# Four units of w_in beside the splitting of x, loaded with it in nine pieces, with squares summed alongside and two raw weight buffers

## The chip, the cores and the metric

The kernel runs on one core of one Trainium2 chip. The metric is the time of one execution on the device in microseconds, the median of three runs. Five engines work side by side and meet only at semaphores: TensorE (PE; PEld is its weight load), VectorE (DVE), ScalarE (ACT), GpSimd (POOL) and SyncE (SP), whose queue issues nearly all loads.

## What is computed

One layer of a decoder for 288 tokens: 256 of a prompt and 8 times 4 of samples, with D = 2048. All of it is fp32. Cut to what matters:

```python
h = rmsnorm(x, g_pre_mix)                 # x * rsqrt(mean(x*x) + eps) * g
z = h @ w_in                              # columns: q | k | v | g_ret | B | C | h_conv | gate_a | gate_b
q, k, v, g_ret, gb, gc, hc, gate_a, gate_b = split(z)
o = retention(rotary(q), rotary(k), v, state_ret)      # 8 heads, per-head decay
y_a = (silu(g_ret) * groupnorm(o)) @ p_ret
y_b = (gb * causal_dwconv(gc * hc)) @ p_conv
m = sigmoid(gate_a) * y_a + sigmoid(gate_b) * y_b
x = x + rmsnorm(m @ w_o, g_post_mix)
h2 = rmsnorm(x, g_pre_ffn)
f = (gelu(causal_dwconv(h2 @ w_up) + b) * (h2 @ w_gate)) @ w_down
x = x + rmsnorm(f, g_post_ffn)
```

## The kernel before

Tokens lie along the free dimension, 288 wide; D lies on partitions, 16 blocks of 128 (k). A *unit* is 128 output columns of a weight matrix, 1 MB, over 16 blocks. To keep fp32 accuracy each operand is split into a high part (fp32r) and a low part, and `mm3` (L118 to 121) makes three matmuls of 128x128 by 128x288 for each block: 48 a unit.

`wunit` (L98 to 114) brings one unit: SP loads it into a tile of the tag raw (the pool has three buffers), ScalarE casts the high part (L110), VectorE subtracts for the low part (L111), in halves of 1024 columns; the tags wh and wl hold three halves each. `gemm` runs mm3 over them, into a PSUM bank of the tag acc (three banks; the tag r has five, L87). `project` (L241) is a unit of w_in, unless its sum already lies in `pre`.

The front (L198 to 239) loads x into xt in five pieces, and with each the same rows of three units, FIRST = (0, 1, 16): two blocks of q and one of k. For each piece ScalarE makes hop's high part x*g (L215), VectorE its low part (L216), the weights are split (L221, L222), and TensorE multiplies. ScalarE squares x (L234), GpSimd adds the squares up (L237, L239) into the first of the tiles acca. Then `rstd_tokens` (three matmuls of the sum with a column, L167; GpSimd's power, L171) starts the first norm, unit 17 is projected, and `rstd_bcast` (VectorE's diagonal L180, fp32 matmuls with a tile of ones, L182, named strb) with ScalarE's copy gives rstd1. The norm's rstd is applied behind the products: cos and sin are multiplied by it (L283, L284), and `v_unit` (L317) multiplies its PSUM sum by it into vT, a product of 256 and one of 32 columns four times over (L322, L323), which frees the bank.

Later come the eight heads with their states (POOL and SP load and store them), w_o (L730, with x1 loaded anew at L693 and 694), the second norm with three first units of w_up and w_gate beside it (L738 to 756; two have tiles of their own for the parts, the third uses `wunit`), and w_down (L869 to 880). A scheduler sets each engine's order of work from its own estimate of times, except in blocks with a hand-written order; on an engine, instructions run in that order.

Of the kernel before, what the change touches and what calls it, by code (L numbers as in the profile page):

```python
# [17 lines left out]
P = 128  # L18
# [58 lines left out]
def tile_hybrid_step(ctx: ExitStack, tc: tile.TileContext, a, o):  # L77
# [20 lines left out]
    def wunit(src, pieces, step=1024):  # L98
        u = n_unit[0]
        n_unit[0] += 1  # L100
        raw = wp.tile([P, 2048], F32, tag="raw", name=f"raw{u}")
        nc.sync.dma_start(out=raw[:, : sum(pieces)], in_=src)
        parts = []
        at = 0
        for i, n in enumerate(pieces):
            wh = wp.tile([P, 1024], F32R, tag="wh", name=f"wh{u}_{i}")
            wl = wp.tile([P, 1024], F32R, tag="wl", name=f"wl{u}_{i}")
            for c in range(0, n, step):
                to, of = slice(c, min(c + step, n)), slice(at + c, at + min(c + step, n))
# [50 lines left out]
    LAST = N - P  # L160
    CHUNKS = ((0, 0, P, 0), (1, P, P, 0), (2, LAST, NS, P - NS))

    def rstd_tokens(sq, name):

        st = psum("r", f"st_{name}")
        for c, at, _, _ in CHUNKS:
            T.matmul(st[:, c : c + 1], sq[:, at : at + P], mean, start=True, stop=True)  # L167
        tt = cp.tile([P, 3], F32, tag="stt", name=f"stt_{name}", bufs=2)
        V.tensor_scalar(out=tt, in0=st[:, 0:3], scalar1=EPS, scalar2=None, op0=ALU.add)
        r = cp.tile([P, 3], F32, tag="str", name=f"str_{name}", bufs=2)  # L170
        G.tensor_tensor(out=r, in0=tt, in1=mhalf[:, 0:3], op=ALU.pow)  # L171
        return r

    def rstd_bcast(r, name):

        dg = cp.tile([P, N], F32, tag="stdg", name=f"stdg_{name}")
        rb = psum("r", f"strb_{name}")
        for c, _, n, skip in CHUNKS:
            to = slice(P * c, P * c + n)
            V.tensor_scalar(out=dg[:, to], in0=ident[:, skip:], scalar1=r[:, c : c + 1],  # L180
                            scalar2=None, op0=ALU.mult)
            T.matmul(rb[:, to], ones, dg[:, to], start=True, stop=True)  # L182
        return rb[:, :N]


    hstack = ExitStack()
    hp = Pool(hstack.enter_context(tc.tile_pool(name="hp", bufs=1)))
    hops = [hp.tile([P, 2, N], F32R, name=f"hop{k}") for k in range(KT)]
    acca = [hp.tile([P, N], F32, name=f"acca{k}") for k in range(KT)]
    rstd1 = hp.tile([P, N], F32, name="rstd1")  # L190


    warm = cp.tile([P, 4], F32, name="warm")
    S.activation(warm, mhalf, AF.Tanh)
    g1 = const("g1", [P, KT])
    pre = {}
    sq_acc = acca[0]
    with tc.tile_pool(name="xp", bufs=1) as xpool:  # L198
        xp = Pool(xpool)
        FIRST = (0, 1, 16)  # L200
        xt = xp.tile([P, KT, N], F32, name="xt")
        raws = [xp.tile([P, 2048], F32, name=f"raw_s{u}") for u in FIRST]
        whs = [xp.tile([P, 2048], F32R, name=f"wh_s{u}") for u in FIRST]
        wls = [xp.tile([P, 2048], F32R, name=f"wl_s{u}") for u in FIRST]
        accs = [psum("r" if i == 0 else "acc", f"a_s{u}") for i, u in enumerate(FIRST)]
        pieces = ((0, 2), (2, 4), (4, 8), (8, 12), (12, 16))
        for k0, k1 in pieces:
            nc.sync.dma_start(out=xt[:, k0:k1, :], in_=a["xT"][:, k0:k1, :])
            w = slice(P * k0, P * k1)
            for raw, u in zip(raws, FIRST, strict=True):  # L210
                nc.sync.dma_start(out=raw[:, w], in_=a["w_in"][u][:, w])
        for k0, k1 in pieces:
            w = slice(P * k0, P * k1)
            for k in range(k0, k1):
                S.activation(hops[k][:, 0, :], xt[:, k, :], AF.Copy, scale=g1[:, k : k + 1])  # L215
                V.scalar_tensor_tensor(  # L216
                    out=hops[k][:, 1, :], in0=xt[:, k, :], scalar=g1[:, k : k + 1],
                    in1=hops[k][:, 0, :].bitcast(F32), op0=ALU.mult, op1=ALU.subtract,
                )
            for i, raw in enumerate(raws):  # L220
                S.copy(whs[i][:, w], raw[:, w])  # L221
                V.tensor_tensor(out=wls[i][:, w], in0=raw[:, w], in1=whs[i][:, w].bitcast(F32),  # L222
                                op=ALU.subtract)
# [6 lines left out]
        for k0, k1 in pieces[1:]:  # L230
            if k0 == 2:
                k0 = 0
            sq = xp.tile([P, 4, N], F32, tag="sq", name=f"sq{k0}", bufs=1)
            S.square(sq, xt[:, k0:k1, :])  # L234
            for j in range(4):
                if k0 == 0 and j == 0:
                    G.tensor_copy(out=sq_acc, in_=sq[:, 0, :])  # L237
                else:
# [602 lines left out]
    for half in range(2):  # L841
# [189 lines left out]
```

## Time and profile before

| | us |
|---|---|
| median of three runs | 2555.78 (2554.3 to 2555.91) |
| the profiled execution | 2555.46 |
| its span, first to last instruction | 2553.4 |
| TensorE busy | 2536.8 (99%) |
| VectorE busy | 1534.6 (60%) |
| ScalarE busy | 1067.8 (42%) |
| GpSimd busy | 90.2 (4%) |
| mean granted clock of TensorE | 0.999 |

The span begins with the first instruction and ends with the last; the profiled execution's own time lies 2.1 us above it. A busy share says how much of the span an engine had an instruction running, not whether it ran at full pace; matmuls overlap in the pipeline, so the distance between two starts, not a duration, is what one costs.

### The profile page before, as it was taken

The numbers are of one execution on the slowest core, as the hardware profiler recorded it, in microseconds if no ns is written. First come the engines' busy times: TensorE is split into PE (matmuls) and PEld (weight loads), VectorE is DVE, ScalarE is ACT, GpSimd is POOL, SyncE is SP. The second block draws the span as 40 slices with busy tenths as digits, with TensorE's granted clock in tenths as the row PEclk, the third lists the DMA queues.
The fourth block names the chain that finished last, engine by engine and source line by source line (L and its number), as shares of the span: only waits on it lengthen the run. The fifth ranks groups of instructions, "written<-read, shape, count | busy, mean of one in ns | idle before, by whom it ended". The sixth has DMA issues, their size and how long they took to land.

```text
span 2553.4 us, 44916 instructions
## 1 busy us (share of the span) xinstructions
PE 2536.8 (99%) x18864; PEld 2480.2 (97%) x18864; DVE 1534.6 (60%) x2339; ACT 1067.8 (42%) x1463; POOL 90.2 (4%) x256
## 2 busy tenths in 40 slices
PE   8999999999999999999999999999999999999998
PEld 8999999999999999999999999999999999999998
DVE  7565656666666666555555554477666446666654
ACT  5444434443444433333333333454444334444443
POOL 2000000000000000000000000021000000000001
PEclk9999999999999999999999999999999999999999
DMA  7465765657565664444444445544444454444645
GB/s 270 174 237 202 245 223 217 242 199 257 207 256 209 237 225 182 165 165 165 168 165 166 166 166 214 207 168 165 166 165 152 167 174 173 166 165 166 222 163 183
DMA packets 90347, 493.06 MB, mean 193 GB/s; under 512 B 11040, under 2 KB 13856, under 8 KB 47776
## 3 DMA queue, kind: packets, MB, share of 16 engines
q1 hardware_dynamic: 88416, 480.74, 52.7%
q0 software_dynamic: 1728, 9.44, 1.0%
q8 instruction: 148, 2.42, 0.4%
q14 instruction: 55, 0.45, 0.1%
HBM read 440.04 MB, written 50.10 MB: 192 GB/s over the span
## 4 chain that ended last, share of the span: by engine, by line
PE 97%; DVE 1%; DMA 1%; issue 0%; ACT 0%; SPq 0%; DVEq 0%; ACTq 0%
PE a_d L121 4%; PE a_d L119 4%; PE a_d L120 4%; PE a_gate L121 4%; PE a_gate L120 4%; PE a_gate L119 4%; PE a_up L121 4%; PE a_up L120 3%; PE a_up L119 3%; PE a_p L119 3%; PE a_g L119 3%; PE a_g L120 3%; PE a_gt L121 3%; PE a_p L121 3%; PE a_g L121 3%; PE a_gt L119 3%
## 5 line engine op out<-in xcount | busy, mean ns | idle before, releaser
L111 DVE TENSOR_TENSOR wl<-raw,wh 128x1024 fp32r<-128x1024 f32 (+2 forms) x776 | 906.2, 1168 | 683.6 <-ACT wh L110 679.5
L110 ACT CAST wh<-raw 128x1024 fp32r<-128x1024 f32 (+2 forms) x776 | 778.1, 1003 | 1279.0 <-PE a_d L120 154.2
L119 PE MATMUL a_d<-fop,wh 128*128 128x288 f32 x704 | 207.9, 295 | 0.0
L120 PE MATMUL a_d<-fop,wh 128*128 128x288 f32 x704 | 207.0, 294 | 0.0
L121 PE MATMUL a_d<-fop,wl 128*128 128x288 f32 x704 | 206.7, 294 | 0.0
L119 PE MATMUL a_gate<-h2op,wh 128*128 128x288 f32 x688 | 203.2, 295 | 0.0
L120 PE MATMUL a_gate<-h2op,wh 128*128 128x288 f32 x688 | 203.0, 295 | 0.0
L121 PE MATMUL a_gate<-h2op,wl 128*128 128x288 f32 x688 | 202.8, 295 | 0.0
L119 PE MATMUL a_up<-h2op,wh 128*128 128x288 f32 x672 | 198.4, 295 | 0.0
L120 PE MATMUL a_up<-h2op,wh 128*128 128x288 f32 x672 | 198.3, 295 | 0.0
L121 PE MATMUL a_up<-h2op,wl 128*128 128x288 f32 x672 | 198.2, 295 | 0.0
L119 PE MATMUL a_p<-yop,wh 128*128 128x288 f32 x512 | 153.1, 299 | 0.0
L119 PE MATMUL a_g<-hop,wh 128*128 128x288 f32 x512 | 152.6, 298 | 0.0
L120 PE MATMUL a_g<-hop,wh 128*128 128x288 f32 x512 | 151.7, 296 | 0.0
L119 PE MATMUL a_v<-hop,wh 128*128 128x288 f32 x512 | 151.2, 295 | 0.0
L119 PE MATMUL a_gt<-hop,wh 128*128 128x288 f32 x512 | 151.1, 295 | 0.0
L120 PE MATMUL a_gt<-hop,wh 128*128 128x288 f32 x512 | 150.9, 295 | 0.0
L120 PE MATMUL a_p<-yop,wh 128*128 128x288 f32 x512 | 150.8, 294 | 0.0
L120 PE MATMUL a_v<-hop,wh 128*128 128x288 f32 x512 | 150.6, 294 | 0.0
L121 PE MATMUL a_gt<-hop,wl 128*128 128x288 f32 x512 | 150.6, 294 | 0.0
L121 PE MATMUL a_p<-yop,wl 128*128 128x288 f32 x512 | 150.5, 294 | 0.0
L121 PE MATMUL a_g<-hop,wl 128*128 128x288 f32 x512 | 150.4, 294 | 0.0
(303 smaller groups left out, 6627.5 us busy)
## 6 DMA issues: line engine op xcount, KB each, us to landing
raw<-in_w_in SPq DMA_DIRECT2D x173, 1024.0 KB, 4.9
raw<-in_w_down SPq DMA_DIRECT2D x64, 704.0 KB, 4.0
raw<-in_w_up SPq DMA_DIRECT2D x43, 1024.0 KB, 4.8
raw<-in_w_gate SPq DMA_DIRECT2D x43, 1024.0 KB, 4.8
st<-in_state SPq DMA_DIRECT2D x64, 512.0 KB, 5.0
out_ret_s<-st SPq DMA_DIRECT2D x64, 512.0 KB, 6.6
raw<-in_p_ret SPq DMA_DIRECT2D x32, 1024.0 KB, 4.8
raw<-in_p_conv SPq DMA_DIRECT2D x16, 1024.0 KB, 4.7
```

What stands on the lines that cost most here:

```text
L110: S.copy(wh[:, to], raw[:, of])
L111: V.tensor_tensor(out=wl[:, to], in0=raw[:, of], in1=wh[:, to].bitcast(F32), op=ALU.subtract)
L119: T.matmul(out, lh, rh, start=first, stop=False)
L120: T.matmul(out, lh, rl, start=False, stop=False)
L121: T.matmul(out, ll, rh, start=False, stop=last)
```

## The change

The front takes four units, 0, 1, 16 and 17, in nine pieces, the first two of one block k, the rest of two. The host puts x's rows and the four units' rows of a piece side by side (`first`), so a piece is one load; the first pieces lie in the room that acca takes later. ScalarE squares x in place three pieces later and VectorE adds the squares four pieces later; the order on both is written by hand. Eight matmuls of a tile of ones with itself stand ahead of all others on TensorE. The load of g1 moves from SP's queue to ScalarE's. Behind the front, v unit 0 of head 0 is projected, then the statistics' matmuls are pinned, v unit 1 is projected, and the broadcast's matmuls are pinned behind it. Every raw tile has two buffers instead of three.

```diff
+FIRST = (0, 1, H * DK // P, H * DK // P + 1)
+PIECES = ((0, 1), (1, 2), (2, 4), (4, 6), (6, 8), (8, 10), (10, 12), (12, 14), (14, 16))
...
-        raw = wp.tile([P, 2048], F32, tag="raw", name=f"raw{u}")
+        raw = wp.tile([P, 2048], F32, tag="raw", name=f"raw{u}", bufs=2)
...
+    def pinned(ins, pin):
+        if pin:
+            tc.keep_in_program_order(ins)
...
-            T.matmul(st[:, c : c + 1], sq[:, at : at + P], mean, start=True, stop=True)
+            pinned(T.matmul(st[:, c : c + 1], sq[:, at : at + P], mean, start=True, stop=True), pin)
...
-            T.matmul(rb[:, to], ones, dg[:, to], start=True, stop=True)
+            pinned(T.matmul(rb[:, to], ones, dg[:, to], start=True, stop=True), pin)
...
-    acca = [hp.tile([P, N], F32, name=f"acca{k}") for k in range(KT)]
+    early = hp.tile([P, KT * N], F32, tag="acca", name="early")
...
+    g1 = cp.tile([P, KT], F32, name="g1")
+    nc.scalar.dma_start(out=g1, in_=a["g1"])
     warm = cp.tile([P, 4], F32, name="warm")
     S.activation(warm, mhalf, AF.Tanh)
-    g1 = const("g1", [P, KT])
...
+        for k0, k1 in PIECES:
+            if ROW * k1 <= KT * N:
+                t = early[:, ROW * k0 : ROW * k1]
+            else:
+                t = xp.tile([P, ROW * (k1 - k0)], F32, name=f"xw{k0}")
+            nc.sync.dma_start(out=t, in_=a["first"][:, ROW * k0 : ROW * k1])
...
+        dummy = psum("r", "warm_up")
+        for i in range(8):
+            T.matmul(dummy[:, :P], ones, ones, start=i == 0, stop=i == 7)
+        accs = [psum("r" if i < 3 else "acc", f"a_s{u}") for i, u in enumerate(FIRST)]
+
+        def squares(i):
+            S.square(loads[i][0], loads[i][0])
+
+        def add_squares(i):
+            x = loads[i][0]
+            for k in range(x.shape[1]):
+                if i == 0 and k == 0:
+                    V.tensor_copy(out=sq_acc, in_=x[:, 0, :])
+                else:
+                    V.tensor_tensor(out=sq_acc, in0=sq_acc, in1=x[:, k, :], op=ALU.add)
+
+        with tc.manual_schedule(engines={mybir.EngineType.DVE, mybir.EngineType.Activation}):
+            for p, ((x, raw), h, w, (k0, k1)) in enumerate(zip(loads, wh, wl, PIECES, strict=True)):
                 for k in range(k0, k1):
+                    S.activation(hops[k][:, 0, :], x[:, k - k0, :], AF.Copy, scale=g1[:, k : k + 1])
+                    V.scalar_tensor_tensor(
...
+                step = 2 if k1 - k0 > 1 else 4
+                for i0 in range(0, NU, step):
+                    u = slice(i0, i0 + step)
+                    S.copy(h[:, u, :], raw[:, u, :])
+                    V.tensor_tensor(out=w[:, u, :], in0=raw[:, u, :], in1=h[:, u, :].bitcast(F32),
+                                    op=ALU.subtract)
...
+                if p >= 3:
+                    squares(p - 3)
+                if p >= 4:
+                    add_squares(p - 4)
...
-            S.square(sq, xt[:, k0:k1, :])
...
-                    G.tensor_tensor(out=sq_acc, in0=sq_acc, in1=sq[:, j, :], op=ALU.add)
...
-    r1 = rstd_tokens(sq_acc, "n1")
-    pre[17] = project(17, "a_s17")
-    S.copy(rstd1, rstd_bcast(r1, "n1"))
+
+    first_v = 2 * H * DK // P
+    pre[first_v] = project(first_v, "a_v0")
+    r1 = rstd_tokens(sq_acc, "n1", pin=True)
+    pre[first_v + 1] = project(first_v + 1, "a_v1")
+    S.copy(rstd1, rstd_bcast(r1, "n1", pin=True))
+    accs_a = hp.tile([P, KT, N], F32, tag="acca", name="acca")
+    acca = [accs_a[:, n, :] for n in range(KT)]
...
-        raw = wp.tile([P, 2048], F32, tag="raw", name=f"raw_d{i}")
+        raw = wp.tile([P, 2048], F32, tag="raw", name=f"raw_d{i}", bufs=2)
...
+    arr["first"] = np.concatenate([
+        t for k0, k1 in PIECES
+        for t in [arr["xT"][:, k0:k1].reshape(P, -1)] + [arr["w_in"][u][:, P * k0 : P * k1] for u in FIRST]
+    ], axis=1)
```

The first place is TensorE's row at the broadcast of the first norm. Names: a_v0_0 is v unit 0 in the kernel before, a_v1 is v unit 1 in the changed one and a_v0_2 unit 2, strb_n1 the broadcast. Before:

```order
L119 MATMUL a_v0_0_522<-hop8_90,wh1_1_518 128x288
L120 MATMUL a_v0_0_522<-hop8_90,wh1_1_518 128x288
L121 MATMUL a_v0_0_522<-hop8_90,wl1_1_519 128x288
L182 MATMUL strb_n1_454<-stdg_n1_453,ones_73 128x128 x2
L182 MATMUL strb_n1_454<-stdg_n1_453,ones_73 128x32
L119 MATMUL a_v0_0_522<-hop9_91,wh1_1_518 128x288
```

The same place on TensorE now:

```order
L123 MATMUL a_v1_516<-hop15_97,wh1_1_512 128x288
L124 MATMUL a_v1_516<-hop15_97,wh1_1_512 128x288
L125 MATMUL a_v1_516<-hop15_97,wl1_1_513 128x288
L190 MATMUL strb_n1_566<-stdg_n1_565,ones_73 128x128 x2
L190 MATMUL strb_n1_566<-stdg_n1_565,ones_73 128x32
L123 MATMUL a_v0_2_639<-hop0_82,wh2_0_631 128x288
```

The broadcast moved from the middle of the first v unit to the end of the second; the matmul behind it opens v unit 2, in the PSUM bank that v unit 0 had.

The second place is VectorE's row from the diagonal (stdg) to the first products with rstd1; wl2 and wl3 are low parts of the third and fourth unit loaded through `wunit`. Before:

```order
L180 TENSOR_SCALAR stdg_n1_453<-ident_68,str_n1_392 128x128 x2
L180 TENSOR_SCALAR stdg_n1_453<-ident_68,str_n1_392 128x32
L111 TENSOR_TENSOR wl2_0_576<-raw2_573,wh2_0_575 128x1024
L111 TENSOR_TENSOR wl2_1_580<-raw2_573,wh2_1_579 128x1024
L283 TENSOR_TENSOR cos_476<-cos_476,rstd1_114 128x288
L284 TENSOR_TENSOR sin_477<-sin_477,rstd1_114 128x288
```

The same stretch of VectorE now:

```order
L188 TENSOR_SCALAR stdg_n1_565<-ident_68,str_n1_504 128x128 x2
L188 TENSOR_SCALAR stdg_n1_565<-ident_68,str_n1_504 128x32
L115 TENSOR_TENSOR wl2_1_636<-raw2_629,wh2_1_635 128x1024
L115 TENSOR_TENSOR wl3_0_693<-raw3_690,wh3_0_692 128x1024
L316 TENSOR_TENSOR cos_589<-cos_589,rstd1_99 128x288
L317 TENSOR_TENSOR sin_590<-sin_590,rstd1_99 128x288
L355 TENSOR_TENSOR vT0_624<-a_v0_449,rstd1_99 128x256
L356 TENSOR_TENSOR vT0_624<-a_v0_449,rstd1_99 128x128
L355 TENSOR_TENSOR vT0_624<-a_v1_516,rstd1_99 128x256
L356 TENSOR_TENSOR vT0_624<-a_v1_516,rstd1_99 128x128
```

The products of v units 0 and 1 now follow cos and sin directly, and the low part of the fourth unit's first half (wl3_0) stands ahead of them.

The third place is SP's queue at the start of the w_o loop; x1 is the reloaded x. Before:

```order
L102 DMA raw221_16784<-in_w_o 128x2048
L102 DMA raw222_16845<-in_w_o 128x2048
L102 DMA raw223_16908<-in_w_o 128x2048
L102 DMA raw224_16971<-in_w_o 128x2048
L694 DMA x1_16761<-in_xT 128x1152 x4
L102 DMA raw225_17034<-in_w_o 128x2048
```

The same place in SP's queue now:

```order
L106 DMA raw220_16779<-in_w_o 128x2048
L106 DMA raw221_16840<-in_w_o 128x2048
L106 DMA raw222_16903<-in_w_o 128x2048
L727 DMA x1_16756<-in_xT 128x1152 x4
L106 DMA raw223_16966<-in_w_o 128x2048
L106 DMA raw224_17029<-in_w_o 128x2048
```

The fourth load of w_o moved from ahead of x1's four loads to behind them.

## Rows read from the trace of the kernel before

**Rows 1.** The page's list of busy time over the whole span (busy us, share of the span, instructions).

```profile
PE 2536.8 (99%) x18864; PEld 2480.2 (97%) x18864; DVE 1534.6 (60%) x2339; ACT 1067.8 (42%) x1463; POOL 90.2 (4%) x256
```

**Rows 2.** What TensorE waited for over the whole span (releaser: us in total, times, longest us).

```profile
PE a_s L119 <- ACT wh_s L221: 5.8, 2, 5.6
PE a_s L121 <- DVE wl_s L222: 2.7, 3, 1.2
```

**Rows 3.** The timeline of TensorE at the start (start us, us, engine, line, operation, tiles; in brackets the idle time before it and what ended it), and behind it one line of the busy time by stretch (window, length, then busy us and records of PE, PEld, DVE, ACT, POOL, then granted clock, DMA share, GB/s).

```profile
5.59 0.61 PE L119 MATMUL a_s<-hop,wh_s 128*128 128x288 f32 x1 [5.59 <-ACT wh_s L221]
...
10.66 0.44 PE L119 MATMUL a_s<-hop,wh_s 128*128 128x288 f32 x1
10.90 0.33 PE L120 MATMUL a_s<-hop,wh_s 128*128 128x288 f32 x1
...
15.27 0.40 PE L121 MATMUL a_s<-hop,wl_s 128*128 128x288 f32 x1 [1.17 <-DVE wl_s L222]
15.51 0.29 PE L119 MATMUL a_s<-hop,wh_s 128*128 128x288 f32 x1
...
20.00 0.30 PE L120 MATMUL a_s<-hop,wh_s 128*128 128x288 f32 x1
...
38.13 0.29 PE L119 MATMUL a_v<-hop,wh 128*128 128x288 f32 x1
...
5.59:10.90 5.31, 5.10 (x20) 4.75 (x20) 3.14 (x8) 3.82 (x9) 1.07 (x2) 1.00 0.96 304
```

**Rows 4.** The timelines of SP, ScalarE, VectorE and GpSimd in the same stretch (columns as before; xN rows hold N instructions of one form).

```profile
1.19 0.42 SPq L208 DMA_DIRECT2D xt<-in_xT  x1
...
4.29 0.96 ACT L215 ACTIVATE hop<-xt,g 128x288 fp32r<-128x288 f32 x2 [2.05 <-DMA xt<-in_xT]
...
4.85 0.95 DVE L216 SCALAR_TENSOR_TENSOR hop<-xt,g,hop 128x288 fp32r<-128x288 f32 x2 [3.83 <-ACT hop L215]
...
12.39 1.12 ACT L221 CAST wh_s<-raw_s 128x512 fp32r<-128x512 f32 x2
...
14.54 1.88 DVE L222 TENSOR_TENSOR wl_s<-raw_s,wh_s 128x512 fp32r<-128x512 f32 x3
...
15.96 4.09 POOL L239 TENSOR_TENSOR acca<-acca,sq 128x288 f32<-128x288 f32 x4 [2.95 <-ACT sq L234]
...
16.35 4.02 DVE L216 SCALAR_TENSOR_TENSOR hop<-xt,g,hop 128x288 fp32r<-128x288 f32 x4
```

**Rows 5.** The timelines of ScalarE, TensorE and VectorE around the first norm's broadcast, and behind them two lines of the tile a_v's own list (its two VectorE readers: ns least/median/most).

```profile
37.87 0.29 PE L120 MATMUL a_s<-hop,wh 128*128 128x288 f32 x1
...
38.20 1.05 ACT L110 CAST wh<-raw 128x1024 fp32r<-128x1024 f32 x1 [2.20 <-PE a_s L120]
...
39.38 1.22 DVE L111 TENSOR_TENSOR wl<-raw,wh 128x1024 fp32r<-128x1024 f32 x1
...
41.70 0.75 PE L182 MATMUL strb_n<-stdg_n,ones 128*128 128x128 f32 x6
...
43.60 0.45 DVE L283 TENSOR_TENSOR cos<-cos,rstd 128x288 f32<-128x288 f32 x1
43.97 0.45 DVE L284 TENSOR_TENSOR sin<-sin,rstd 128x288 f32<-128x288 f32 x1
...
L322 DVE TENSOR_TENSOR vT<-a_v,rstd x32: 415/424/426, 45.7 to 876.7; 128x256 f32<-128x256 f32 x32
L323 DVE TENSOR_TENSOR vT<-a_v,rstd x32: 278/280/284, 46.1 to 877.1; 128x128 f32<-128x128 f32 x32
```

**Rows 6.** The weight loads: what the page and the DMA views give for them (tiles, queue, how many, KB each, median us from issue to landing; first two of the whole span, then of the load issued at 1587.59), then SP's and ScalarE's timelines in the w_o loop.

```profile
raw<-in_w_in SPq DMA_DIRECT2D x173, 1024.0 KB, 4.9
...
out_ret_s<-st SPq DMA_DIRECT2D x64, 512.0 KB, 6.6
...
raw<-in_w_o SPq DMA_DIRECT2D x1, 1024.0 KB, 14.8
...
1583.15 1.81 SPq L694 DMA_DIRECT2D x<-in_xT  x4
1587.59 0.33 SPq L102 DMA_DIRECT2D raw<-in_w_o  x1
...
1594.72 1.05 ACT L110 CAST wh<-raw 128x1024 fp32r<-128x1024 f32 x1 [2.12 <-PE a_o L120]
```

**Rows 7.** The w_down stage just after the cache rows are loaded: the load in the DMA view of 2397 to 2397.3 (columns as in the group before), its issue on SP's timeline, and a cast on ScalarE's.

```profile
raw<-in_w_down SPq DMA_DIRECT2D x1, 704.0 KB, 9.2
...
2397.06 0.33 SPq L102 DMA_DIRECT2D raw<-in_w_down  x1
...
2401.74 0.83 ACT L110 CAST wh<-raw 128x768 fp32r<-128x768 f32 x1 [1.25 <-PE a_d L120]
```

**Rows 8.** VectorE's timeline around the second norm's chain.

```profile
1681.05 1.29 DVE L111 TENSOR_TENSOR wl<-raw,wh 128x512 fp32r<-128x512 f32 x2 [0.71 <-ACT wh L110]
...
1685.71 0.16 DVE L169 TENSOR_SCALAR stt_n<-st_n 128x3 f32<-128x3 f32 x1 [1.10 <-PE st_n L167]
1686.86 0.64 DVE L180 TENSOR_SCALAR stdg_n<-ident,str_n 128x128 f32<-128x128 f32 x3 [0.99 <-POOL str_n L171]
```

**Rows 9.** Busy time by stretch after the last matmul of the program (columns as in group 3's last line; the granted clock is the third number from the end).

```profile
2545.90:2550.00 4.10, 0.00 (x0) 0.00 (x0) 0.96 (x2) 0.56 (x1) 0.00 (x0) 1.00 1.03 386
2550.00:2551.00 1.00, 0.00 (x0) 0.00 (x0) 0.00 (x0) 0.00 (x0) 0.00 (x0) 0.74 0.94 368
```

More of the change, by code (lines that the diff above doesn't have):

```diff
@@ L161, in tile_hybrid_step, with rstd_tokens @@
     CHUNKS = ((0, 0, P, 0), (1, P, P, 0), (2, LAST, NS, P - NS))
-    def rstd_tokens(sq, name):
+    def pinned(ins, pin):
+        if pin:
+            tc.keep_in_program_order(ins)
+    def rstd_tokens(sq, name, pin=False):
         st = psum("r", f"st_{name}")
         for c, at, _, _ in CHUNKS:
-            T.matmul(st[:, c : c + 1], sq[:, at : at + P], mean, start=True, stop=True)
+            pinned(T.matmul(st[:, c : c + 1], sq[:, at : at + P], mean, start=True, stop=True), pin)
         tt = cp.tile([P, 3], F32, tag="stt", name=f"stt_{name}", bufs=2)
@@ L172, in rstd_tokens, with rstd_bcast @@
         return r
-    def rstd_bcast(r, name):
+    def rstd_bcast(r, name, pin=False):
         dg = cp.tile([P, N], F32, tag="stdg", name=f"stdg_{name}")
@@ L188, in tile_hybrid_step @@
     hops = [hp.tile([P, 2, N], F32R, name=f"hop{k}") for k in range(KT)]
-    acca = [hp.tile([P, N], F32, name=f"acca{k}") for k in range(KT)]
+    early = hp.tile([P, KT * N], F32, tag="acca", name="early")
     rstd1 = hp.tile([P, N], F32, name="rstd1")
+    g1 = cp.tile([P, KT], F32, name="g1")
+    nc.scalar.dma_start(out=g1, in_=a["g1"])
     warm = cp.tile([P, 4], F32, name="warm")
     S.activation(warm, mhalf, AF.Tanh)
-    g1 = const("g1", [P, KT])
     pre = {}
-    sq_acc = acca[0]
+    NU = len(FIRST)
@@ L198, in tile_hybrid_step @@
+    ROW = N + NU * P
     with tc.tile_pool(name="xp", bufs=1) as xpool:
         xp = Pool(xpool)
[L200 to L223, printed above, removed]
-                for k in range(k0, k1):
-                    c = slice(P * k, P * k + P)
-                    mm3(accs[i][:, :N], whs[i][:, c], wls[i][:, c], hops[k][:, 0, :], hops[k][:, 1, :],
-                        k == 0, k == KT - 1)
+        loads = []
@@ new lines, in tile_hybrid_step @@
+        for k0, k1 in PIECES:
[4 more added lines that the diff above has]
+            nc.sync.dma_start(out=t, in_=a["first"][:, ROW * k0 : ROW * k1])
+            loads.append((t[:, : N * (k1 - k0)].rearrange("p (k n) -> p k n", n=N),
+                          t[:, N * (k1 - k0) :].rearrange("p (u c) -> p u c", u=NU)))
+        wh = [xp.tile([P, NU, P * (k1 - k0)], F32R, name=f"wh_s{k0}") for k0, k1 in PIECES]
@@ new lines, in tile_hybrid_step @@
+        wl = [xp.tile([P, NU, P * (k1 - k0)], F32R, name=f"wl_s{k0}") for k0, k1 in PIECES]
+        sq_acc = xp.tile([P, N], F32, name="sq_acc")
+        dummy = psum("r", "warm_up")
[11 more added lines that the diff above has]
+                    V.tensor_tensor(out=sq_acc, in0=sq_acc, in1=x[:, k, :], op=ALU.add)
@@ new lines, in tile_hybrid_step @@
+        with tc.manual_schedule(engines={mybir.EngineType.DVE, mybir.EngineType.Activation}):
+            for p, ((x, raw), h, w, (k0, k1)) in enumerate(zip(loads, wh, wl, PIECES, strict=True)):
+                for k in range(k0, k1):
+                    S.activation(hops[k][:, 0, :], x[:, k - k0, :], AF.Copy, scale=g1[:, k : k + 1])
+                    V.scalar_tensor_tensor(
+                        out=hops[k][:, 1, :], in0=x[:, k - k0, :], scalar=g1[:, k : k + 1],
+                        in1=hops[k][:, 0, :].bitcast(F32), op0=ALU.mult, op1=ALU.subtract,
+                    )
+                step = 2 if k1 - k0 > 1 else 4
[4 more added lines that the diff above has]
+                                    op=ALU.subtract)
+                    for i in range(i0, min(i0 + step, NU)):
+                        for k in range(k0, k1):
+                            c = slice(P * (k - k0), P * (k - k0) + P)
+                            mm3(accs[i][:, :N], h[:, i, c], w[:, i, c], hops[k][:, 0, :], hops[k][:, 1, :],
+                                k == 0, k == KT - 1)
+                if p >= 3:
+                    squares(p - 3)
+                if p >= 4:
+                    add_squares(p - 4)
+            for p in range(len(PIECES) - 3, len(PIECES)):
+                squares(p)
+                add_squares(p - 1)
+            add_squares(len(PIECES) - 1)
@@ L228, in tile_hybrid_step @@
         for i, u in enumerate(FIRST):
             pre[u] = accs[i]
[L230 to L233, printed above, removed]
-            S.square(sq, xt[:, k0:k1, :])
[L235 to L238, printed above, removed]
-                    G.tensor_tensor(out=sq_acc, in0=sq_acc, in1=sq[:, j, :], op=ALU.add)
@@ L886, in tile_hybrid_step @@
     lent = [h2_lend(0, "kv_v", 4), h2_lend(1, "kv_1", 6), h2_lend(2, "kv_2", 6)]
-    raws = [wp.tile([P, 2048], F32R, tag="raw", name=f"kv_r{i}").rearrange("p (i d) -> p i d", d=DV)
+    raws = [wp.tile([P, 2048], F32R, tag="raw", name=f"kv_r{i}", bufs=2).rearrange("p (i d) -> p i d", d=DV)
             for i in range(2)]
```

## The prediction

> **What bounds the kernel now.** The list of busy time comes first: TensorE has 2536.8 us of the 2553.4 us span, VectorE 60%, ScalarE 42% [rows 1]. So only what TensorE idles, or spends at half its clock, can be won or lost, and some 17 us in all are open to that. TensorE's waits say where they lie: two items of any size, 5.8 us for the first cast and 2.7 us for VectorE's low parts, both inside the three units beside the splitting of x [rows 2]. Last its timeline at the start: the first matmul is at 5.59, the starts lie 0.24 us apart until 10.90, and from 15.51 to 20.00 there are 34 of them, 0.132 us apart (a unit of 48 takes 6.33) [rows 3]. The two paces are the engine's two clock levels, 1.2 and 2.4 GHz; the granted clock stands at 1.00 in both stretches, so here the pace is the witness and not that column.
>
> What is lost before the first v unit starts at 38.13: 192 matmuls at 0.132 us are 25.3 us, the three small matmuls of the statistics about 0.6, so 12.25 us are lost [rows 3]. Of these 5.59 lie before the first matmul. Between 5.59 and 10.90 there are 20 matmuls, 2.64 us of work in 5.31: 2.67 lost. The other 4.0 are gaps while VectorE is late, 1.17 us the longest [rows 3].
>
> **The change part by part.**
>
> *1. The front: −6.5.* (a) The first load now carries one k of x and of four units, 410 KB. Before, the first x piece was issued at 1.19 and was there at 4.29, 3.1 us later [rows 4]; the new load is issued about 0.75, since nothing stands ahead of it, so at 3.85 or a little after. Then a split of x (0.48) and a cast of 512 columns (0.56) [rows 4]: TensorE starts between 4.8 and 5.3, I take 5.2. (b) The eight dummy matmuls need only the tile of ones and can begin near 1.1. Their price I bound by the broadcast's fp32 matmuls, about 0.6 to 0.75 us for 288 columns at the full clock [rows 5]: 1024 columns are 4.2 to 5.3 us at the half clock, so they end with or just after the first cast. Full pace came 5.3 us after the first matmul before [rows 3]; counted from 1.1 it comes about 6.4, which leaves 1.2 us at half pace, 0.6 lost. (c) After that a two-k piece is 24 matmuls, 3.16 us. VectorE needs 2×0.47 + 2×0.6 + 2×0.37 = 2.75, ScalarE 2×0.45 + 2×0.56 + 0.6 = 2.6 [rows 4, 5]; both are less, so TensorE leads. That VectorE's row of four splits took 4.02 us instead of 1.9 stood beside GpSimd's adds (15.96 to 20.05 and 16.35 to 20.37) [rows 4]; those adds are gone from GpSimd and VectorE carries them. So gaps are 0 to 0.4. Sum: 5.2 + 0.6 = 5.8 lost instead of 12.25, −6.5; from −5 (first load as slow as 4.6 us, some gaps) to −7.3 (cast at 4.6, clock already up). The load of g1 on ScalarE's queue costs nothing: it has 3 us under the first load.
>
> *2. The pinned broadcast: +3.15.* Before, the broadcast stood in the middle of the first v unit, and whatever waited for rstd1 had half a unit of cover. Now it stands behind two v units, and TensorE's next matmul, of v unit 2, writes the PSUM bank from which v unit 0 must first be multiplied by rstd1. In VectorE's row that product stands behind the low part of unit 3's first half, cos and sin. That low part waits for ScalarE's cast, which waits for the last read of its buffer, the last L120 of v unit 1. The rows of before have each step: from the start of such an L120 to the cast 0.33 (37.87 to 38.20), cast 1.05, low part 1.22 (1.17 to the next start), cos 0.37, sin 0.36, the two products 0.42 and 0.28, some hand-over: 4.0 us [rows 5]. TensorE has in that time its last matmuls and the broadcast, 0.85. So it idles 3.15 (2.9 to 3.4). The rest of the chain (VectorE's adds, GpSimd's power) has v unit 1, 6.33 us, as cover and costs nothing.
>
> *3. Two raw buffers, steady state: 0.* A load is issued when the low part that last read its buffer is done, about 2.4 us after the cast before it (38.20 to 40.60) [rows 5], and with two buffers its own cast comes three halves (3×3.17) after that same cast: 7.1 us for the landing. TensorE waits only 6.33 + 0.26 − 1.05 − 0.08 − 1.22 = 4.24 us after the cast could have begun. So a load may take 7.1 us for nothing and 11.3 before TensorE stops; a lone one takes 4.9 [rows 6]. Where loads share the queues it counts:
>
> *4. w_o, +3.45.* The fourth w_o load moves from before the four loads of x1 to behind them. What is issued there now was issued at 1587.59 and took 14.8 us beside x1 and the cached rows [rows 6]: it landed at 1602.39. The cast of the unit that would need it was at 1594.72 [rows 6]: 7.7 us late, less 4.24. Lower end 2 (x1 issued sooner), upper 4.5.
>
> *5. w_down beside the cache rows, +1.8.* The load issued at 2397.06 took 9.2 us, to 2406.26; it now serves the unit whose cast was at 2401.74 [rows 7]: 4.5 late. With 704 columns the cover is 2.74 (4.33 + 0.26 − 0.83 − 0.08 − 0.94, the casts from the row, the low part 1.22 scaled). Range 0.2 to 2.2.
>
> *6. Second norm, +0.8.* One first unit's load is issued one place later, so its low parts of 0.6 us, two of which now stand between the statistics' copy and the diagonal, delay a chain that runs from 1685.71 to 1686.86 with little cover [rows 8]: 0 to 1.5.
>
> *7. Heads, +0.25.* State loads and stores share the queues with weights; 6.6 us for a store of 512 KB beside them [rows 6] shows loads near 7 to 11 us there, mostly inside the cover of step 3. 0, or up to 8 if the mix gets worse.
>
> The last loads, one unit later at the end, have 14 us of cover: 0. Sum: −6.5 + 3.15 + 3.45 + 1.8 + 0.8 + 0.25 = +2.95. The profiled run took 2555.46 us, 0.3 under the median of 2555.78; 2555.46 + 2.95 = 2558.4, against the median 2558.7. I say **2558.5**.
>
> **Rivals.** *A: the buffers cost nothing.* If the fourth w_o load lands early because x1's loads are issued earlier, and the others fit, only steps 1 and 2 count: −3.35, 2552.3. For: a lone load has 6 us to spare. Against: the 14.8 us of that very place [rows 6].
>
> *B: the front alone.* If the wait of step 2 is absent as well (products reordered behind another bank), −6.5: 2549.2, faster. Against: VectorE's row is read from the changed program's order.
>
> *C: slower, the clock.* The pauses of steps 2 and 4 are the first of over 3 us in a stream that has none above 1.2. If TensorE falls to 1.2 GHz in each, it loses the 2.67 us of the front again [rows 3], twice: 2558.5 + 5.3 = 2563.8. It decides from the point where a pause is long enough for the clock to fall. Against: after the last matmul, at 2545.8, the granted clock stood at 1.00 through 2550 and fell to 0.74 in the next us [rows 9], so it outlasted 4.1 us of idleness, more than either pause. The Trainium skill ("TensorE: Matmul & The Clock Gate", section "Why this matters for your kernels") says the opposite of what those rows show for a pause of this size: an idle gap between matmul bursts sends the engine back to the half clock. By that rule the sum is 2563.8; by the row it is 2558.5, and I go by the row.
>
> *D: slower, the heads.* With two buffers each of the eight heads has loads issued beside four state loads and stores; if each comes 1 us over the 11.3, eight us more, 2566.5. It decides where a load of the mix takes over 11.3 us. SP is held by stores in the heads too, so a weight load behind them is issued late.
>
> **How the numbers follow.** Something near the sum (2555 to 2561): 0.56. A: 0.15. B: 0.05. C: 0.11. D: 0.13. No change to a measurement is 0.2%, 5.1 us: from 2550.7 to 2560.9. Faster: B and a corner of A, 0.08. Slower: C, D and the sum's upper edge, 0.26. Same: 0.66. The range takes in A's upper half (front weaker) and C: 2553 to 2565, leaving out B and most of D.
>
> **What would show it.** Right: first x matmul at 4.8 to 5.3, pace 0.13 from about 6.4, the first v unit (now ahead of the statistics) at about 31; one wait of 3 us of TensorE behind the broadcast, for VectorE's vT; one of about 3.5 in the w_o loop for the cast whose load landed near 1602; one near 2 in w_down. Wrong: matmul starts 0.24 apart after any of these pauses (C), waits for raw loads in the heads (D), or no wait in the w_o loop (A). The forecast fails most easily on steps 4 and 7, whose landings depend on how queues share; on step 1 if the dummies end after 5.3 and hold the first real matmul.

## The result and the profile after

| | us |
|---|---|
| before, median of 6 runs | 2555.07 (2554.3 to 2555.91) |
| changed, median of 6 runs | 2563.72 (2562.09 to 2567.6) |
| ratio, 95% interval | 1.0036 (1.0026 to 1.0046) |
| the changed kernel's profiled execution, its span | 2562.09, 2560.3 |

The change makes the kernel slower by 0.36%. The forecast of 2558.5 is 5.2 us too low; the time lies in its range, on its upper side, and 0.1 us from the time worked out for rival C. The profiled execution is the fastest of the six, 1.6 us under their median, so what follows accounts for a span longer by 6.9 us; what the other executions lose beyond that is in no trace.

TensorE's waits in the changed kernel (releaser: us in total, times, longest us), where [rows 2] showed two of the front:

```profile
PE a_v L123 <- DVE vT L356: 3.0, 1, 3.0
PE a_o L123 <- ACT wh L114: 3.0, 1, 3.0
PE warm_up L225 <- DVE mean L163: 1.1, 1, 1.1
PE to L566 <- DVE sm L393: 1.0, 1, 1.0
PE strb_n L190 <- DVE stdg_n L188: 0.9, 1, 0.9
PE a_d L125 <- DVE wl L115: 0.9, 2, 0.5
PE a_s L123 <- ACT wh_s L250: 0.8, 1, 0.8
PE a_o L125 <- DVE wl L115: 0.4, 1, 0.4
```

The 5.8 us ahead of the first cast are 1.1 and 0.8 now, with the dummy matmuls between them; the first real matmul is no sooner for it, at 5.62 against 5.59. But two waits of 3.0 us have come, at the two places where the prediction had them. These waits sum to some 11 us against 8.5 in [rows 2]; that difference doesn't explain a span longer by 6.9. Where the rest is, the offsets of like instructions say: pairing VectorE's instructions of the same tiles in order, the changed trace against that of before (medians, + is later). An offset says how much later a place is reached than before, a step how much the stretch up to it added.

| place | offset, us | step | what it is made of |
|---|---|---|---|
| first v unit starts | −6.0 | −6.0 | 31.48 against 38.13, which has 0.6 of statistics ahead of it |
| 60 to 100 us | −1.1 | +4.9 | pause behind the broadcast 3.03, and 1.8 |
| 200 to 1500 us | −0.6 | +0.6 | first head, "to" waits for the scores' product |
| 1615 to 1655 us | +5.9 | +6.4 | w_o: waits 2.97 and 0.41, and 3.0 |
| 1730 to 2000 us | +6.3 | +0.4 | second norm |
| 2420 to 2500 us | +7.9 | +1.6 | w_down beside the cache rows |
| end of the span | +6.9 | −1.0 | what follows the last matmul is 1.0 shorter |

Behind two pauses stand 1.8 and 3.0 us that are no wait. Busy time by stretch in the changed kernel, around the first pause and around the second (window, length, busy us and records of PE, PEld, DVE, ACT, POOL, granted clock, DMA share, GB/s):

```profile
44.80:48.70 3.90, 0.87 (x9) 0.79 (x8) 2.67 (x6) 1.94 (x4) 0.00 (x0) 1.00 0.93 300
48.70:50.00 1.30, 1.30 (x9) 1.30 (x10) 1.30 (x4) 0.00 (x0) 0.00 (x0) 0.91 1.03 419
50.00:51.00 1.00, 1.00 (x6) 1.00 (x5) 1.00 (x3) 0.00 (x0) 0.00 (x0) 0.50 1.03 422
...
52.00:53.00 1.00, 1.00 (x6) 1.00 (x6) 1.00 (x5) 0.00 (x0) 0.00 (x0) 0.50 0.98 418
53.00:54.00 1.00, 1.00 (x8) 1.00 (x8) 0.54 (x2) 0.45 (x1) 0.00 (x0) 0.91 0.59 238
...
1600.00:1602.00 2.00, 0.61 (x5) 0.37 (x3) 0.46 (x1) 0.80 (x2) 0.00 (x0) 1.00 1.07 414
1602.00:1604.00 2.00, 0.42 (x2) 0.42 (x2) 0.44 (x1) 1.52 (x2) 0.00 (x0) 0.71 0.95 375
1604.00:1606.00 2.00, 1.59 (x7) 1.24 (x7) 1.92 (x2) 0.73 (x2) 0.00 (x0) 0.50 0.15 61
...
1608.00:1610.00 2.00, 2.00 (x11) 2.00 (x10) 0.05 (x1) 0.00 (x0) 0.00 (x0) 0.58 1.00 418
```

Between 50 and 53 the granted clock is 0.50, the 1.2 GHz level: TensorE is busy all the time, but its matmuls start 0.24 us apart from 49.88 to 53.00 and 0.13 apart before and behind. (The counts in the rows, 6 instead of 8 in a microsecond, take in every matmul that reaches into the stretch, so they show less than the full difference.) By the shares in the rows the clock falls near 49.8, about 4.1 us after the pause began (45.6) and 1.1 us after work has resumed (48.67), and comes back near 53.2, 3.4 us later. At w_o it falls inside the pause, near 1602.8, and is back only near 1609.7. A busy share of 1.00 hides all of this; the granted clock and the distance of the starts show it.

VectorE's and ScalarE's timelines at the first pause, and TensorE's, answer to [rows 5]:

```profile
44.89 0.75 PE L190 MATMUL strb_n<-stdg_n,ones 128*128 128x128 f32 x6
48.67 0.37 PE L123 MATMUL a_v<-hop,wh 128*128 128x288 f32 x1 [3.03 <-DVE vT L356]
...
44.95 1.04 ACT L114 CAST wh<-raw 128x1024 fp32r<-128x1024 f32 x1 [2.07 <-PE a_v L124]
45.91 0.39 ACT L282 COPY rstd<-strb_n 128x288 f32<-128x288 f32 x1
...
46.03 1.22 DVE L115 TENSOR_TENSOR wl<-raw,wh 128x1024 fp32r<-128x1024 f32 x1 [1.89 <-ACT wh L114]
47.17 0.45 DVE L316 TENSOR_TENSOR cos<-cos,rstd 128x288 f32<-128x288 f32 x1
47.54 0.45 DVE L317 TENSOR_TENSOR sin<-sin,rstd 128x288 f32<-128x288 f32 x1
47.91 0.42 DVE L355 TENSOR_TENSOR vT<-a_v,rstd 128x256 f32<-128x256 f32 x1
48.24 0.28 DVE L356 TENSOR_TENSOR vT<-a_v,rstd 128x128 f32<-128x128 f32 x1
```

The chain is the forecast one: cast 44.95, low part 46.03, cos, sin, two products, and TensorE at 48.67. rstd1 was there at 46.3, but VectorE took it up at 47.17, behind the low part.

At w_o, from SP's queue, the DMA view and ScalarE's timeline, which answer to [rows 6]:

```profile
1582.60 1.75 SPq L727 DMA_DIRECT2D x<-in_xT  x4
1587.04 32.08 SPq L106 DMA_DIRECT2D raw<-in_w_o  x5
...
raw<-in_w_o SPq DMA_DIRECT2D x1, 1024.0 KB, 15.4
...
1602.48 1.99 ACT L114 CAST wh<-raw 128x1024 fp32r<-128x1024 f32 x2 [1.03 <-DMA raw<-in_w_o]
```

The fourth load is issued at 1587.04 behind x1, takes 15.4 us and lands at 1602.44; the cast follows at once, and the first matmul of that unit is at 1603.58.

### The profile page after: what moved, and what is told of

Same layout as the page of the kernel before. It is cut to its first block, busy times and chain, and to the rows that moved or that the text cites. A ratio compares the mean times of both kernels' runs of the same rounds, so it can differ in the third digit from the quotient of the medians.

```text
span 2560.3 us, 44892 instructions
## 1 busy us (share of the span) xinstructions
PE 2542.2 (99%) x18880; PEld 2485.6 (97%) x18880; DVE 1531.6 (60%) x2354; ACT 1065.7 (42%) x1467; POOL 76.0 (3%) x240
## 4 chain that ended last, share of the span: by engine, by line
PE 92%; issue 4%; DMA 2%; DVE 1%; ACT 0%; POOL 0%; SPq 0%; DVEq 0%; ACTq 0%; POOLq 0%
PE a_d L125 4%; PE a_d L123 4%; PE a_d L124 4%; PE a_gate L125 4%; PE a_gate L124 4%; PE a_gate L123 4%; PE a_up L125 3%; PE a_up L124 3%; PE a_up L123 3%; PE a_p L123 3%; PE a_gt L125 3%; PE a_p L125 3%; PE a_gt L123 3%; PE a_g L123 3%; PE a_g L124 3%
## 5 line engine op out<-in xcount | busy, mean ns | idle before, releaser
L124 PE MATMUL a_d<-fop,wh 128*128 128x288 f32 x704 | 207.0, 294 | 0.0
L124 PE MATMUL a_gate<-h2op,wh 128*128 128x288 f32 x688 | 202.9, 295 | 0.0
L124 PE MATMUL a_up<-h2op,wh 128*128 128x288 f32 x672 | 198.3, 295 | 0.0
L124 PE MATMUL a_g<-hop,wh 128*128 128x288 f32 x512 | 151.7, 296 | 0.0
L124 PE MATMUL a_v<-hop,wh 128*128 128x288 f32 x512 | 151.3, 296 | 0.0
L125 PE MATMUL a_v<-hop,wl 128*128 128x288 f32 x512 | 151.2, 295 | 0.0
L124 PE MATMUL a_gt<-hop,wh 128*128 128x288 f32 x512 | 150.9, 295 | 0.0
L124 PE MATMUL a_p<-yop,wh 128*128 128x288 f32 x512 | 150.8, 295 | 0.0
```

## The experiments

The theory after the result: two buffers and the pinned broadcast make the pauses where forecast, and TensorE pays for a pause twice, as idle time and as half clock behind it. Rivals: the w_o pause is x1's traffic whatever the buffers; the new front disturbs later loads; the slow matmuls behind a pause wait for late parts, not for the clock.

**Three raw buffers**, in all three places where the changed kernel asks for two. To fit, the second two-k piece (the third, in the expectation's words) was halved, which brings the load of its first half into the room of acca:

```diff
-PIECES = ((0, 1), (1, 2), (2, 4), (4, 6), (6, 8), ...
+PIECES = ((0, 1), (1, 2), (2, 4), (4, 5), (5, 6), (6, 8), ...
-        raw = wp.tile([P, 2048], F32, tag="raw", name=f"raw{u}", bufs=2)
+        raw = wp.tile([P, 2048], F32, tag="raw", name=f"raw{u}")
```

> The changed kernel with three raw buffers again; to find the room, its third two-k piece (4,6) becomes two one-k pieces, which then lie in the room of acca. Theory (the loss is made in the places where two buffers run out, each pause paid twice, once as idle time and once as half clock): the steps at w_o (+6.4), the second norm (+0.4) and w_down (+1.6) go, 2563.7 - 8.4 = about 2555.3, with the pause of 3 us behind the broadcast still there. Rival (the w_o pause comes of x1's loads beside the cached rows whatever the buffers are): the w_o pause stays, 2561 or more.

Measured: 2553.06 us (2550.71 to 2554.52), ratio to before 0.999 (0.9981 to 0.9999). Only the pause behind the broadcast is left (3.0). All offsets after the first head stay where they are, −0.5 to −1.0 to the end: the steps at w_o, the second norm and w_down are gone. The buffers are what costs there; x1's traffic alone isn't. It came out 2 us under the expectation; the first head's wait for sm, for which I had not reckoned a part, is missing here too: the head gains 1.2 us, where the changed kernel lost 0.6.

**Two raw buffers in the kernel before**, three places with `bufs=2`, nothing else.

> The kernel before with two raw buffers and nothing else. Theory: a pause of about 3.4 us in the w_o loop, half clock after it, and 0.4 and 1.6 us at the second norm and in w_down, 2555.1 + 8.4 = about 2563.5. Rival (the buffers are harmless, the new front is what disturbs later loads): 2555 to 2557.

Measured: 2566.01 us (2565.07 to 2571.52), ratio 1.0045 (1.0032 to 1.0059). The new front isn't needed for the loss, which is 2.5 us above the expectation. In this run's profile w_o adds 5.5 us, w_down 1.6, and the first head 7.2 of its own. ScalarE's, VectorE's and SP's timelines in that head, and TensorE's and SP's waits (over the whole span):

```profile
158.89 0.34 SPq L484 DMA_DIRECT2D st<-in_state  x1
159.33 0.38 SPq L102 DMA_DIRECT2D raw<-in_w_in  x1
...
165.73 1.04 ACT L110 CAST wh<-raw 128x1024 fp32r<-128x1024 f32 x1 [5.99 <-DMA raw<-in_w_in]
...
166.81 1.23 DVE L111 TENSOR_TENSOR wl<-raw,wh 128x1024 fp32r<-128x1024 f32 x1 [4.76 <-ACT wh L110]
167.95 0.28 DVE L360 TENSOR_TENSOR sm<-sc,mask 128x128 f32<-128x128 f32 x1
...
PE to L533 <- DVE sm L360: 4.5, 2, 3.7
SPq L484 <- DMA out_ret_s<-st: 204.5, 58, 8.9
```

SP holds the weight load behind a state load that itself waits for a store's landing (the last line: 58 state loads do so in this run); the weight load is issued at 159.33, lands at 165.6, ScalarE's cast and VectorE's low part follow, and behind that low part in VectorE's row stands the scores' product (sm), for which TensorE's "to" waits 3.7 us. TensorE stops not for the late weights but for a small product queued behind them. Half clock follows (169.3 to 172.7).

**x1's loads behind the fifth to eighth load of w_o**, two buffers kept:

```diff
-    for q in range(4):
-        nc.sync.dma_start(out=x1[:, 4 * q : 4 * q + 4, :], in_=a["xT"][:, 4 * q : 4 * q + 4, :])
...
     for n in range(KT):
...
+        if 4 <= n < 8:
+            q = n - 4
+            pinned(nc.sync.dma_start(out=x1[:, 4 * q : 4 * q + 4, :], in_=a["xT"][:, 4 * q : 4 * q + 4, :]), True)
```

> The changed kernel with x1's four loads pinned one by one behind the fifth to eighth load of w_o, two raw buffers kept. Theory: the fourth w_o load is issued at 1587 without x1 ahead of it, its landing is under 11.3 us and the pause goes with its half clock, 2563.7 - 6.4 = about 2557.3. Rival (it is the cached rows beside it, not x1's place, or the later loads only take over the wait): a pause of 1 to 3 us stays at the fourth or moves to the sixth load, 2560 to 2564.

Measured: 2558.55 us (2555.85 to 2559.71), ratio 1.0009 (1.0 to 1.0018). The w_o step is 0.0 and no wait has taken its place there. In this run w_down costs 3.7 instead of 1.6, a wait of 1.12 and one of 0.46 with half clock behind them (TensorE's timeline, and a stretch's busy time):

```profile
2406.26 0.40 PE L123 MATMUL a_d<-fop,wh 128*128 128x288 f32 x1 [1.12 <-ACT wh L114]
2407.26 0.40 PE L125 MATMUL a_d<-fop,wl 128*128 128x288 f32 x1 [0.46 <-DVE wl L115]
...
2408.00:2410.00 2.00, 2.00 (x11) 2.00 (x10) 0.96 (x1) 0.83 (x1) 0.00 (x0) 0.50 0.53 127
```

**The broadcast sooner**, in v unit 1 instead of behind it:

```diff
-    pre[first_v + 1] = project(first_v + 1, "a_v1")
-    S.copy(rstd1, rstd_bcast(r1, "n1", pin=True))
+    parts1 = wunit(a["w_in"][first_v + 1], HALVES)
+    acc1 = psum("acc", "a_v1")
+    for i, ((h1, l1), x1h) in enumerate(zip(parts1, hops, strict=True)):
+        if i == 8:
+            S.copy(rstd1, rstd_bcast(r1, "n1", pin=True))
+        mm3(acc1[:, :N], h1, l1, x1h[:, 0, :], x1h[:, 1, :], i == 0, i == KT - 1)
+    pre[first_v + 1] = acc1
```

> The changed kernel with the broadcast of the first norm pinned in v unit 1 (it comes to stand nine matmuls before its end) instead of behind it; in VectorE's row cos, sin and the products of v units 0 and 1 then stand ahead of the low part of the fourth unit. Theory: the pause of 3.0 us shrinks under 1 us and the clock does not fall, so 2 to 2.6 us of idleness and 1.8 us of half clock go, 2559.0 to 2559.9. Rival (the pause alone costs, what follows it is no clock): 2561 to 2561.7.

Measured: 2561.21 us (2558.39 to 2563.2), ratio 1.0022 (1.0014 to 1.0031): less gain in the median than expected, and inside the rival's range, so the median doesn't tell the two apart. The place itself does: the first v unit starts at 30.92 (−6.6), and between 60 and 100 us the offset is −5.25, so the pause and its half clock together cost 1.4 instead of 4.9. This run's profiled execution then loses 6.7 at w_o and more than the changed kernel at the second norm and w_down (1.5 and 2.3 against 0.4 and 1.6).

**Dummy matmuls in both pauses**, eleven in each, with no reader:

```diff
     S.copy(rstd1, rstd_bcast(r1, "n1", pin=True))
+    fill = psum("r", "fill_v")
+    for i in range(11):
+        pinned(T.matmul(fill[:, :P], ones, ones, start=i == 0, stop=i == 10), True)
...
         parts = wunit(a["w_o"][n], HALVES)
+        if n == 3:
+            fill = psum("r", "fill_o")
+            for i in range(11):
+                pinned(T.matmul(fill[:, :P], ones, ones, start=i == 0, stop=i == 10), True)
```

> The changed kernel with eleven matmuls of the tile of ones with itself pinned into each of the two long pauses, behind the broadcast and ahead of the fourth unit of w_o; nothing waits for their result. They take about 2.6 us, less than the pause, so no work comes sooner by them. Theory (the clock falls because of the pause): the waits end when they did, the matmuls behind them run at full pace, and 1.8 + 3.0 us go, about 2558.9. Rival (the slow matmuls behind the pauses come of late low parts and casts, not of the clock): no change, 2562 to 2565.

Measured: 2560.67 us (2557.07 to 2565.18), ratio 1.0027 (1.0017 to 1.0037); on the median alone undecided. The places decide. TensorE's timeline and the stretches behind both pauses:

```profile
46.77 2.70 PE L285 MATMUL fill_v<-ones 128*128 128x128 f32 x22
49.97 0.37 PE L123 MATMUL a_v<-hop,wh 128*128 128x288 f32 x1 [0.50 <-DVE vT L359]
...
51.00:53.00 2.00, 2.00 (x17) 2.00 (x17) 2.00 (x6) 0.00 (x0) 0.00 (x0) 1.00 1.05 426
...
1607.68 0.40 PE L123 MATMUL a_o<-mop,wh 128*128 128x288 f32 x1 [0.20 <-ACT wh L114]
1608.00:1612.00 4.00, 3.27 (x25) 3.06 (x24) 3.13 (x3) 1.62 (x2) 0.00 (x0) 1.00 0.29 63
```

The real matmul still comes when VectorE, or at w_o ScalarE, releases it, and behind it the clock is 1.00 at both places; at the first there are 17 records in 2 us, where the changed kernel had 10 from 50 to 52. From the v unit to 60 us this kernel loses 3.3 instead of 4.9, at w_o 3.9 instead of 6.4. So the slow matmuls were the clock's doing, and idleness brought it down: the half clock costs about 1.6 us behind the first pause and 2.5 behind w_o's. What is left of the 1.8 and 3.0 is no clock and stays when the pause is filled. The median holds more than these two places: this profiled execution, 4.1 us above it, waits 3.4 us for sm in the first head, in the way shown above, and has half clock behind it, 5.2 us in all. How much of that the other executions have isn't recorded.

**No dummy matmuls ahead of the front**, the eight of the changed kernel taken out.

> The changed kernel without the eight matmuls ahead of all others. Theory: the first real matmul is at 5.6 as now, half pace until about 10.9 instead of full pace from 6.2, so 2 to 2.6 us more, 2565.7 to 2566.3. Rival (the pace comes up with the first real matmuls just as soon, or TensorE was waiting for the pieces anyway): 2563 to 2564.5.

Measured: 2567.49 us (2562.38 to 2569.06), ratio 1.0046 (1.0033 to 1.0059). That is above the expected range, but the five executions spread over 6.7 us and the interval overlaps the changed kernel's, so the median leaves it undecided. In its profiled execution, the fastest of the five, the first v unit starts at 33.78, 2.3 later than in the changed kernel. It also holds a case against my theory's letter: the pause behind the broadcast is there in full, and no half clock follows. The place costs 3.3 us here (from the front's offset to 60 us) and 4.9 in the changed kernel, so this too puts the half clock at 1.6.

```profile
50.93 0.37 PE L123 MATMUL a_v<-hop,wh 128*128 128x288 f32 x1 [3.04 <-DVE vT L353]
...
51.00:52.00 1.00, 1.00 (x8) 1.00 (x9) 1.00 (x4) 0.00 (x0) 0.00 (x0) 1.00 1.03 422
52.00:54.00 2.00, 2.00 (x17) 2.00 (x16) 2.00 (x5) 0.00 (x0) 0.00 (x0) 1.00 1.05 438
```

**Three buffers and the early broadcast together.**

> Three raw buffers (as the run with them) and the broadcast nine matmuls before the end of v unit 1: the front alone with neither pause. Theory: 2555.1 - 6 + under 1 + 0.6 at the first head = 2549.5 to 2551.5, faster than before. Rival (something else of the front eats its 6 us, so the parts do not add up): 2553 to 2555.

Measured: 2549.09 us (2548.37 to 2554.7), ratio 0.9981 (0.9972 to 0.999): faster than before, just under the expected range, and 14.6 us under the changed kernel's median. TensorE waits but for this:

```profile
PE warm_up L225 <- DVE mean L163: 1.1, 1, 1.1
PE a_v L123 <- DVE vT L361: 0.6, 1, 0.6
PE a_s L123 <- ACT wh_s L250: 0.5, 1, 0.5
```

Without a long pause its granted clock stays at 1.00 until the last matmul is done; so it does in the three runs that follow with the early broadcast, whose longest wait behind the front is 1.3 us.

**Two buffers, x1 late and the early broadcast.**

> Two raw buffers, x1's loads behind the fifth to eighth load of w_o, and the broadcast nine matmuls before the end of v unit 1. Theory: both pauses gone, the second norm's 0.4 and w_down's 1.6 left: 2563.7 - 6.4 - 4.2 = about 2553.1. Rival (w_o still pauses): 2556 to 2560.

Measured: 2554.49 us (2551.43 to 2560.09), ratio 1.0 (0.9991 to 1.0009). Both pauses are gone; w_down's step of 2.0 and the first head's 1.3 us wait remain. The kernel with the third buffer is some 5 us faster still.

**Ten dummy matmuls, and none**, in the kernel with three buffers and the early broadcast.

> The kernel with three raw buffers and the early broadcast, with ten dummy matmuls instead of eight, so that they reach to the first real matmul and the 0.5 to 0.8 us of idleness between them go. Theory (that idleness sometimes keeps the clock down): full pace from about 6.2 in every execution, about 1.5 us less than the same with eight, 2547.5, and a narrower spread. Rival (when the clock rises is not set by the gap): as with eight, 2548.4 to 2551, or 0.2 us more.

> The same kernel without dummy matmuls: half pace from 5.5 to about 11, where eight dummies gave full pace at 6.2 to 10.8. Theory: 1 to 2.5 us more than with eight, 2550 to 2551.6. Rival (the front is held by its pieces and not by the clock): 2549.

Measured: ten 2549.72 us (2547.57 to 2553.71), ratio 0.9983 (0.9974 to 0.9992); none 2551.42 us (2550.46 to 2552.21), ratio 0.9986 (0.9977 to 0.9995). Against 2549.09 with eight: neither the 2547.5 nor the narrower spread came, so the gap ahead of the first real matmul decides nothing that shows in the median. The dummies together are worth about 2 us in the medians (2551.42 to 2549.72 and 2549.09), with more spread; the intervals overlap. Their starts (ten, then none):

```profile
6.45 0.70 PE L124 MATMUL a_s<-hop,wh_s 128*128 128x288 f32 x4
6.98 0.69 PE L125 MATMUL a_s<-hop,wl_s 128*128 128x288 f32 x4
...
7.00 1.16 PE L124 MATMUL a_s<-hop,wh_s 128*128 128x288 f32 x4
7.96 1.16 PE L125 MATMUL a_s<-hop,wl_s 128*128 128x288 f32 x4
```

The four matmuls of L124 take 0.53 us to the next row at full pace (ten), 0.96 at half (none); without dummies full pace comes at 11.8.

**The eight dummies in the kernel before.**

> The kernel before with the eight dummy matmuls ahead of its three units and nothing else. Theory: its first matmuls wait for casts and low parts as much as for the clock (20 matmuls between 5.59 and 10.90 in 4.75 us of half pace), so 0 to -2 us, 2553 to 2555. Rival (the clock was all that was lost there): -2.7, 2552.

Measured: 2553.14 us (2552.3 to 2557.3), ratio 0.9996 (0.9987 to 1.0005). The median is 1.6 us lower, inside the expectation, but the interval doesn't exclude no change; in the profiled execution (2554.85) the front ends 0.4 later than before, with waits of 2.7 us for VectorE's low parts.

## Why the prediction came out as it did

*Where the time goes* held: both long waits came in the places and by the chains that were read from the order and the rows.

*Step 1, the front: −6.5, measured −6.0* in the profiled execution. The first matmul was at 5.62, not 5.2, and no sooner than before: the first piece took 3.6 us where the sum had 3.1, and the first split of x started at 4.53, released not by the piece but by g1's load, which landed 0.17 later and had been put at nothing:

```profile
4.53 0.53 ACT L242 ACTIVATE hop<-early,g 128x288 fp32r<-128x288 f32 x1 [1.85 <-DMA g<-in_g]
```

Full pace came with the first matmuls, not at 6.4: their starts are 0.13 apart from 5.86 (the 6.2 in the expectations is the start of a row of four). So the gain lies behind the first matmul, where 0.6 us are lost instead of 6.7. That pace was partly chance: in the profiled executions of the seven other kernels with dummies and this front it came with the first matmuls in three and only between 9.2 and 10.7 in four, and the first v unit started between 30.92 and 33.40. So the term was right for one execution and some 1 us too large on the mean of those seen.

*Step 2, the pinned broadcast: +3.15, measured 3.03.* Right in chain and size; the place costs 0.2 more than the wait even where no half clock follows.

*Step 4, w_o: +3.45, measured 2.97 + 0.41 = 3.38.* Right; 15.4 us to landing where 14.8 were taken.

*Steps 5 and 6: +1.8 and +0.8, measured 1.6 and 0.4.* Right in place, the second mis-sized. That the first came out so near is partly luck: not one wait near 2 for a cast came, as forecast, but two of 0.46 and 0.47 for low parts of two units, at 2408.84 and 2414.05, each some 0.75 us with the slow start behind it.

*Step 7, the heads: +0.25, measured +0.6*, and mis-sized in spread: with two buffers the first head cost 5.2 us in one execution of another kernel and 7.2 in one of the kernel before with two buffers. Rival D's place was right but its price was put on all heads and on the loads themselves; what stops TensorE is sm, which stands behind the late low part in VectorE's row, and in the first head.

*The step that failed is rival C's dismissal.* I put it at 0.11 because the granted clock stood at 1.00 for 4.1 us after the last matmul [rows 9]. That row shows how late the clock falls after idleness begins. It doesn't show that a pause shorter than this is free, and the sign named for C, starts 0.24 apart behind the pauses, is what came. Behind the first pause the clock fell 4.1 us after the pause's start, 1.1 us after TensorE had resumed; at w_o it fell 2.2 us after the pause's start. What is no wait came to 1.8 and 3.0, together 4.8, and by the run with filled pauses about 4.0 of it (1.6 and 2.5) is the clock, where rival C had 5.3; that run shows, in one execution, that idleness is the cause. Without the half clock the profiled execution would lie near 2558.1, by subtraction, close to the forecast. That the median lies 0.1 us from rival C's 2563.8 is luck: C's price was 1.3 too high, and the median is 1.6 above the execution in which it was measured. The rule of the Trainium skill ("TensorE: Matmul & The Clock Gate", section "Why this matters for your kernels") that an idle gap of this size between matmul bursts sends the clock back to the half level agrees with these traces at 9 of the 10 pauses of 2.7 to 3.7 us in the profiled executions (the tenth is in the run without dummies).

*What the prediction had no term for:* the tail behind the last matmul, 1.0 us shorter than before in this execution. It is 6.6 to 8.3 us long in the profiled executions of all kernels here, 7.5 before, so the difference lies within what executions vary by.

*Chances.* Slower had 0.26, same 0.66: the right mechanisms with one price left out put the likeliest class on the wrong side of 0.2%. The time lies in the range only because the range was drawn to take in rival C.

Open: why the same pause is followed by half clock in one execution and not in another. No run tells this apart; the changed kernel's spread of 5.5 us against 1.6 of the kernel before is compatible with it, and with the first head's wait, which varies as well.

## What to carry to other kernels

A buffer taken away is not judged by the steady state, where a load here had over 6 us to spare, but at each place where another transfer joins or jumps the queue: there the load's landing, as the trace of before has it for the next place in the queue, less the cover, is the pause. At w_o it was read ahead to a tenth (3.45 against 3.38); in w_down the sum came near, but as two short waits.

A pause of some microseconds in a dense stream of matmuls has a second price behind it, so count half-clock time for each new long wait. The 2.67 us that the front of the same kernel shows were the upper end here, 1.6 and 2.5 were paid. Look for it in the granted clock and the distance of the starts, not in the busy share. And follow small products in an engine's row: what waits is often queued behind a late weight part rather than late itself.

## What was not expected of the hardware

The clock's fall and rise are not the same from one execution to the next: after the same eight dummy matmuls (1.06 to 4.8 us) the real ones ran at full pace from the start in the changed kernel and only from 10.7 in the one with three buffers, as TensorE's timelines show (the changed kernel, then that one; the first four take 0.63 us to the next row, then 1.13):

```profile
5.62 0.79 PE L123 MATMUL a_s<-hop,wh_s 128*128 128x288 f32 x4 [0.78 <-ACT wh_s L250]
6.25 0.69 PE L124 MATMUL a_s<-hop,wh_s 128*128 128x288 f32 x4
...
5.60 1.33 PE L123 MATMUL a_s<-hop,wh_s 128*128 128x288 f32 x4 [0.75 <-ACT wh_s L250]
6.73 0.68 PE L124 MATMUL a_s<-hop,wh_s 128*128 128x288 f32 x2
```

A pause of 3.04 us was followed by no fall in one execution, and waits of 1.12 and 0.46 by 3.4 us of half clock in another (x1 late), while waits of 1.14 and 0.46 at the same place were followed by none in a third (the early broadcast). The clock can fall a microsecond after work has resumed (pause to 48.67, fall near 49.8).
